# Placing a decoder trunk's buffers at multiples of 512 bytes, with raw pairs at a pitch of 272 columns

## The chip, the cores and the metric
The kernel runs on one core of a Trainium2 chip. A core has a matrix engine (PE, with its weight loads listed apart as PEld), a vector engine (DVE), a scalar engine (ACT), a general engine (POOL) and a queue engine (SP) that here issues every DMA. The metric is the device time of one launch in microseconds. Three runs of the kernel before took 624.08, 625.19 and 625.38 us, so the median is 625.19 us.

## The reference
A trunk of two layers over 256 positions of 1,024 features, in float32. Layer 0 mixes positions by causal attention with 8 heads of 128 (with 256 positions there is one block, so the block-sparse routing selects nothing beyond it), layer 1 by a gated causal convolution of width 3. After each mixer comes a SwiGLU with 2,816 hidden features. Each of the four sub-layers reads a normed and modulated residual and adds its result under a gate; shift, scale and gate come from the conditioning vector `c`.

```python
sc = silu(c)
for i in range(2):
    sh_m, sc_m, g_m, sh_f, sc_f, g_f = split(sc @ w_ada[i] + b_ada[i], 6)
    h = rms_norm(x, norm_mix[i]) * (1 + sc_m) + sh_m
    y = attention(h, w_qkv, w_o, q_gain, k_gain) if i == 0 else short_conv(h, w_in, conv_w, w_out)
    x = x + g_m * y
    h = rms_norm(x, norm_ffn[i]) * (1 + sc_f) + sh_f
    x = x + g_f * ((silu(h @ W_gate) * (h @ W_up)) @ w_down[i])
```

## The kernel before
The residual stands feature-major in `xT`: 8 tiles of 128 features by 256 positions. Every large product is made in three passes (`mm3`, lines 285 to 289): each float32 operand is split into a float32r part `h` and a remainder `l`, and PE computes h·h, h·l and l·h into the same accumulators. A pass is one matmul of a 128 by 128 block that PE loads and 256 columns that it streams; lines 287, 288 and 289 are the three passes of all large products.

The weights come in chunks of 1,024 rows by 256 columns (1 MB). SP loads a chunk into one of five buffers `wf`; ACT copies it into `wh` and DVE subtracts to get `wl` (lines 98 and 99), in two halves each, three buffers of both kinds. The list `chunks` sets their order; between them run the pieces of the modulation matrices (`wa`), which DVE multiplies and sums up (line 116). A scheduler places the instructions of the engines, except in the first stage, whose order is written by hand.

The stages in order of time: a first stage with the first modulation, queries and half of the keys (to some 57 us); keys, values and the attention's own steps; the output product `op_o`; the gate and up products of layer 0 (`pg`, `pu`, with the modulated pair `f0h`, `f0l`); the down products `op_d` (with the pair `a0h`, `a0l`, 22 rows); in layer 1 the convolution's products (`pc`, `pu`, `pb`, with `m1h`, `m1l`), `op_co`, and again gate, up and down (`f1`, `a1`).

The first products of three sub-layers don't wait for the norm. `Norm.take` writes a raw pair row by row as the residual's tiles come: 256 positions times scale, without the norm, and two more columns that hold the shift (lines 373 to 381). A row therefore has 258 columns, and the raw pair lies in the memory of `av` or of the wide pair: `raw_in` and `wide_pair` cut it out with rows of S + 2 columns. `raw_gemm` multiplies it, computes the norm's sum in between (lines 387 and 388) and applies it afterwards.

Tiles are placed in the order of their first use, one pool after the other, at multiples of 32 bytes in each partition. The constants before the weight pool end such that the first `wf` buffer starts at byte 20,448. Modulo 512, all `wf`, `wh` and `wl` buffers start at 480. The modulated pair (`m0`, `f0`, `m1`, `f1`: the same memory) starts at 32 in both halves, `a0h` and `a1h` at 96, `a0l` and `a1l` at 480, the wide pair (`ov`, `zv`) at 480 and 32, `xT` at 32. `ident_r`, with which `keep_warm` (line 566) keeps PE occupied early, starts at 256.

Of the kernel before, what the change touches and what calls it, by code (L numbers as in the profile page):

```python
# [8 lines left out]
F32 = mybir.dt.float32  # L9
# [6 lines left out]
P = 128  # L16
S = 256
D = 1024
KD = D // P
# [4 lines left out]
KF = D_FF // P  # L24
CW = 256
EPS = 1e-6
MASKED = -1e30
# [4 lines left out]
def trunk_kernel(ctx: ExitStack, tc: tile.TileContext, x, c, w_ada, b_ada, norm_mix, norm_ffn, w_qkv, w_o,  # L32
# [3 lines left out]
    const = ctx.enter_context(tc.tile_pool(name="const", bufs=1))  # L36
# [16 lines left out]

# [1 line left out]
    crow = const.tile([KD, P], F32, name="crow")  # L55
# [24 lines left out]

# [1 line left out]
    def load(src, nk, ncol, name):  # L82
# [17 lines left out]

# [1 line left out]
    mod = const.tile([P, DEPTH * 48], F32, name="mod")  # L102
    acc_of = {}
    late, gets = [], [0]

    def ada_piece(l, part, i):
        w = load(w_ada[l, i * 256:(i + 1) * 256, part * D:(part + 1) * D], 2, D, f"wa_{l}_{part}_{i}")
        if i == 0:
            acc_of[l, part] = tmp.tile([P, D], F32, tag="acc", name=f"acc_{l}_{part}", bufs=1)
        acc = acc_of[l, part]  # L110
        for kk in range(2):
            k = 2 * i + kk
            if k == 0:
                nc.vector.tensor_scalar(acc, w[:, kk], sc[:, k:k + 1], None, op0=ALU.mult)
            else:
                nc.vector.scalar_tensor_tensor(acc, w[:, kk], sc[:, k:k + 1], acc, op0=ALU.mult, op1=ALU.add)  # L116
        if i < 3:
            return
        if l == 0 and part != G_F:
            late.append((gets[0], lambda: ada_end(l, part, acc)))  # L120
            return
        # the sum over the partitions, of three bfloat16 parts that add up to the float32 values: less for PE
        parts = [tmp.tile([P, D], BF16, tag=f"part{n}", name=f"part{n}_{l}_{part}", bufs=1) for n in range(3)]
        for n, p in enumerate(parts):
            if n < 2:
                nc.scalar.activation(p, acc, AF.Copy)
                nc.vector.tensor_sub(acc if n == 0 else parts[2], acc, p)
        late.append((gets[0], lambda: ada_end_parts(l, part, parts)))

    def ada_end(l, part, acc):  # L130
        # the sum over the partitions, on four groups of 32 columns of the array at once: less for DVE and ScalarE
        ps = ps_misc(f"mod_ps_{l}_{part}")[:, :2 * P]
        for g in range(4):
            nc.tensor.matmul(ps[32 * g:32 * g + 32], one.to_broadcast([P, 32]), acc[:, g * 2 * P:(g + 1) * 2 * P],
                             start=True, stop=True, skip_group_check=True, tile_position=(0, 32 * g))
        y = tmp.tile([P, 2, P], F32, tag="t", name=f"mod_y_{l}_{part}", bufs=3)
        nc.scalar.activation(y, ps.rearrange("p (i c) -> p i c", c=P), AF.Copy)

        def end():
            ps = ps_misc(f"mod_c_{l}_{part}")  # L140
            for i in range(2):
                nc.tensor.transpose(ps[:, i * P:(i + 1) * P], y[:, i], ident)
            mod_from(ps[:, :2 * P].rearrange("p (i g r) -> p g i r", i=2, r=32)[:, :, :, 0], l, part)

        return end
# [43 lines left out]
    brow, vrow, grow = (rows[:n, i * P:(i + 1) * P] for i, n in enumerate((DEPTH * 48, 42, 16)))  # L189
    x_flat = act.tile([P, KD * (S + 2)], F32, tag="zh", name="x_tok")  # L190
    x_tok = x_flat[:, :2 * D].rearrange("p (t d) -> p t d", d=D)
# [16 lines left out]

# [1 line left out]
    chunks = []  # L210
# [72 lines left out]

# [1 line left out]
    def mm3(ps, lhs, rhs, first, last):  # L285
# [28 lines left out]

    # A raw pair holds x * (1 + scale) * gain, not yet over its norm, and the shift as one more token (twice, for an
    # even number of them). Products of it need no norm; rstd and the product of the shift come to them afterwards:
    # (x A rstd + sh) W = (x A) W rstd + sh W.
    RAW = KD * (S + 2)

    def wide_pair(name):  # L320
        flat = [act.tile([P, RAW], F32R, tag="z" + p, name=name + p) for p in "hl"]
        return (tuple(f[:, :KD * S].rearrange("p (k s) -> p k s", s=S) for f in flat),
                tuple(f.rearrange("p (k s) -> p k s", s=S + 2) for f in flat))

    def raw_in(pair):
        flat = [t.rearrange("p k s -> p (k s)") for t in pair]
        return tuple(f[:, KF * S - RAW:].rearrange("p (k s) -> p k s", s=S + 2) for f in flat)

# [1 line left out]
    xT = act.tile([P, KD, S], F32, name="xT")  # L330
# [20 lines left out]
    class Norm:  # L351
        """Sums of squares over the features, gathered as the residual's tiles come."""

# [83 lines left out]
    def raw_gemm(keys, norm, name):  # L437
        """Two chunks' products of the raw pair; returns (product * rstd, the shift's product) of each, and
        the modulated pair. The norm's own products come in between."""
        raw = norm.raw  # L440
        ada_ends()
        pss = [[psum.tile([P, S + 2], F32, tag=tag, name=f"raw_{name}_{i}{o}", bufs=n) for o in range(2)]
               for i, (tag, n) in enumerate((("gemm", 4), ("alt", 2)))]
        ws = [get(k) for k in keys]
        for k in range(KD):
            if k == 2:
                norm.rstd()
            if k == 4:
                rows = norm.rows()
                with tc.high_priority(400):  # L450
                    hs = modulated(norm.l, norm.sh, norm.scl, rows, name)
            for ps, (wh, wl) in zip(pss, ws):
                for o in range(2):
                    cs = slice(o * P, (o + 1) * P)
                    mm3(ps[o], (wh[:, k, cs], wl[:, k, cs]), (raw[0][:, k], raw[1][:, k]), k == 0, k == KD - 1)
        res = []
        for i, tag in enumerate("sa"):
            y = tmp.tile([P, 2, S], F32, tag=tag, name=f"rawy_{name}_{i}")
            b = tmp.tile([P, 2], F32, tag="rawb", name=f"rawb_{name}_{i}")
            for o in range(2):  # L460
                nc.vector.tensor_copy(b[:, o:o + 1], pss[i][o][:, S:S + 1])
                nc.vector.tensor_mul(y[:, o], pss[i][o][:, :S], rows)
            res.append((y, b))
        return res[0], res[1], hs
# [19 lines left out]

# [1 line left out]
    def mod_sums(w, name):  # L486
        # Four groups of 32 columns of the array hold four rows of c at once: partial sums in four groups of partitions.
        n = w.shape[1]
# [10 lines left out]
    def group_sums(ps, y, name):  # L499
        # the four groups' partial sums added up, as columns  # L500
        n = y.shape[1]
# [48 lines left out]
    def first_products(k, ops, js):  # L550
        wh, wl = ops
        for j in js:
            for t in range(2):
                ts = slice(t * P, (t + 1) * P)
                # q feature-major, k token-major
                if j < 4:
# [9 lines left out]
    def keep_warm(n):  # L566
        # The array's clock falls while it idles: products that nothing reads keep it up until the first operands are there.
        ps = ps_misc("warm")
# [4 lines left out]
    with tc.manual_schedule(engines={mybir.EngineType.PE, mybir.EngineType.DVE, mybir.EngineType.Activation}):  # L573
# [4 lines left out]
        nc.vector.tensor_copy(mask_r, causal)  # L578
        # brings the table of square roots in before the first one is needed
        std = const.tile([P, 2], F32, name="std0")  # L580
# [55 lines left out]

# [1 line left out]
    qT = act.tile([P, 2, H, S], F32, tag="ah", name="qkT")  # L638
# [25 lines left out]
    def q_sums(ps, a):  # L664
        # Four heads at once, on 32 columns of the array each: their sums end in four groups of partitions.
        for g in range(4):
# [73 lines left out]

    # The attention's own steps run between the products of the k and v chunks, each late enough to find its operands.
    ahead = get(("k", 2))
# [37 lines left out]

# [1 line left out]
    ups = [act.tile([P, 2, S + 2], F32, tag=f"up{i}", name=f"up{i}") for i in range(2)]  # L782
# [37 lines left out]

# [1 line left out]
    of = out[0].rearrange("(t p) d -> p t d", p=P)  # L822
# [43 lines left out]
```

## Time and profile before
| what | value |
|---|---|
| median of 3 runs | 625.19 us (624.08 to 625.38) |
| span of the profiled execution, from first to last instruction | 622.1 us |
| PE busy, share of the span | 609.7 us, 98% |
| DVE busy | 473.6 us, 76% |
| ACT busy | 323.1 us, 52% |
| DMA | 156.07 MB, mean 251 GB/s |

Busy time of PE is from the start of a matmul to its end, and matmuls overlap: one takes about 280 ns, but the next starts some 115 ns after it. What a stage costs is therefore read from the starts, or from how many matmuls lie in a window. The chain of waits names, from the end backwards, what each step waited for. The span leaves out what lies before the first and after the last instruction; the median of the runs is 3.1 us above it.

### The profile page before, as it was taken

The numbers are of one execution on the slowest core, as the hardware profiler recorded it, in microseconds if no ns is written. First come the engines' busy times: TensorE is split into PE (matmuls) and PEld (weight loads), VectorE is DVE, ScalarE is ACT, GpSimd is POOL, SyncE is SP. The second block draws the span as 40 slices with busy tenths as digits, with TensorE's granted clock in tenths as the row PEclk, the third lists the DMA queues.
The fourth block names the chain that finished last, engine by engine and source line by source line (L and its number), as shares of the span: only waits on it lengthen the run. The fifth ranks groups of instructions, "written<-read, shape, count | busy, mean of one in ns | idle before, by whom it ended". The sixth has DMA issues, their size and how long they took to land.

```text
span 622.1 us, 12512 instructions
## 1 busy us (share of the span) xinstructions
PE 609.7 (98%) x5291; PEld 595.8 (96%) x5291; DVE 473.6 (76%) x668; ACT 323.1 (52%) x518; POOL 19.2 (3%) x26
## 2 busy tenths in 40 slices
PE   7999999999999999999999999999999999999997
PEld 5789999999999999999999999998999999999997
DVE  5567999989989899979888989658976467644440
ACT  5335977466655455535355745545744435533330
POOL 0000000020000000000110000012000000000000
PEclk9999999999999999999999999999999999999999
DMA  9999999966699999798998497646388677655200
GB/s 271 329 331 354 385 370 335 303 219 223 210 323 322 347 333 335 257 318 303 319 302 278 133 304 241 210 138 205 108 299 271 201 225 235 204 188 178 94 18 17
DMA packets 127455, 156.07 MB, mean 251 GB/s; under 512 B 2822, under 2 KB 114856, under 8 KB 127400
## 3 DMA queue, kind: packets, MB, share of 16 engines
q1 hardware_dynamic: 127400, 155.28, 75.6%
q8 instruction: 41, 0.67, 0.5%
q14 instruction: 14, 0.11, 0.1%
HBM read 154.22 MB, written 1.05 MB: 250 GB/s over the span
## 4 chain that ended last, share of the span: by engine, by line
PE 88%; DMA 3%; DVE 3%; issue 3%; ACT 1%; SPq 0%; POOLq 0%; POOL 0%; ACTq 0%
PE pu L289 7%; PE pu L288 7%; PE op_d L287 7%; PE pu L287 7%; PE op_d L289 7%; PE op_d L288 7%; PE pg L289 6%; PE pg L288 6%; PE pg L287 6%; DMA wa<-in_w_ada_dram 2%; DMA wf_qk<-in_w_qkv_dram 1%; PE pv L287 1%; PE pb L288 1%; PE pv L289 1%; PE pb L287 1%
## 5 line engine op out<-in xcount | busy, mean ns | idle before, releaser
L116 DVE SCALAR_TENSOR_TENSOR acc<-wa,sc,acc 128x1024 f32<-128x1024 f32 x70 | 89.8, 1283 | 8.8 <-DMA wa<-in_w_ada_dram 7.5
L98 ACT ACTIVATE wh_d<-wf_d 128x1024 fp32r<-128x1024 f32 (+1 forms) x48 | 45.5, 981 | 69.7 <-issue 47.2
L99 DVE TENSOR_TENSOR wl_d<-wf_d,wh_d 128x1024 fp32r<-128x1024 f32 (+1 forms) x48 | 53.6, 1144 | 30.7 <-ACT wh_d L98 30.5
L98 ACT ACTIVATE wh_u<-wf_u 128x1024 fp32r<-128x1024 f32 x44 | 44.3, 1051 | 45.3 <-issue 34.5
L98 ACT ACTIVATE wh_g<-wf_g 128x1024 fp32r<-128x1024 f32 x44 | 45.5, 1050 | 40.7 <-issue 40.7
L99 DVE TENSOR_TENSOR wl_u<-wf_u,wh_u 128x1024 fp32r<-128x1024 f32 x44 | 52.7, 1233 | 14.0 <-ACT wh_u L98 14.0
L99 DVE TENSOR_TENSOR wl_g<-wf_g,wh_g 128x1024 fp32r<-128x1024 f32 x44 | 54.5, 1245 | 2.1 <-ACT wh_g L98 2.0
L287 PE MATMUL op_d<-a1h,wh_d 128*128 128x256 f32 x176 | 50.3, 286 | 0.0
L287 PE MATMUL op_d<-a0h,wh_d 128*128 128x256 f32 x176 | 50.2, 285 | 0.0
L289 PE MATMUL op_d<-a1h,wl_d 128*128 128x256 f32 x176 | 50.0, 284 | 0.0
L289 PE MATMUL op_d<-a0h,wl_d 128*128 128x256 f32 x176 | 50.0, 284 | 0.0
L288 PE MATMUL op_d<-a1l,wh_d 128*128 128x256 f32 x176 | 49.6, 282 | 0.0
L288 PE MATMUL op_d<-a0l,wh_d 128*128 128x256 f32 x176 | 49.5, 281 | 0.0
L289 PE MATMUL pg<-f1h,wl_g 128*128 128x256 f32 x160 | 44.8, 280 | 0.0
L289 PE MATMUL pu<-f1h,wl_u 128*128 128x256 f32 x160 | 44.8, 280 | 0.0
L287 PE MATMUL pg<-f1h,wh_g 128*128 128x256 f32 x160 | 44.6, 279 | 0.0
L288 PE MATMUL pg<-f1l,wh_g 128*128 128x256 f32 x160 | 44.6, 279 | 0.0
L287 PE MATMUL pu<-f1h,wh_u 128*128 128x256 f32 x160 | 44.6, 279 | 0.0
L288 PE MATMUL pu<-f1l,wh_u 128*128 128x256 f32 x160 | 44.6, 279 | 0.0
L287 PE MATMUL pg<-f0h,wh_g 128*128 128x256 f32 x160 | 44.5, 278 | 0.0
L289 PE MATMUL pg<-f0h,wl_g 128*128 128x256 f32 x160 | 44.4, 278 | 0.0
L289 PE MATMUL pu<-f0h,wl_u 128*128 128x256 f32 x160 | 44.4, 278 | 0.0
(315 smaller groups left out, 2103.6 us busy)
## 6 DMA issues: line engine op xcount, KB each, us to landing
wa<-in_w_ada_dram SPq DMA_DIRECT2D x40, 1024.0 KB, 6.1
wf_g<-in_w_gate_up_dram SPq DMA_DIRECT2D x22, 1024.0 KB, 6.6
wf_u<-in_w_gate_up_dram SPq DMA_DIRECT2D x22, 1024.0 KB, 7.5
wf_d<-in_w_down_dram SPq DMA_DIRECT2D x16, 1024.0 KB, 6.3
wa<-in_w_ada_dram SPq DMA_DIRECT2D x16, 512.0 KB, 7.1
wf_d<-in_w_down_dram SPq DMA_DIRECT2D x8, 768.0 KB, 5.7
wf_qk<-in_w_qkv_dram SPq DMA_DIRECT2D x8, 512.0 KB, 8.1
wf_v<-in_w_qkv_dram SPq DMA_DIRECT2D x4, 1024.0 KB, 7.5
```

The lines of the kernel that those rows point to most:

```text
L98: nc.scalar.activation(wh[:, a:b], wf[:, a:b], AF.Copy)
L99: nc.vector.tensor_sub(wl[:, a:b], wf[:, a:b], wh[:, a:b].bitcast(F32))
L116: nc.vector.scalar_tensor_tensor(acc, w[:, kk], sc[:, k:k + 1], acc, op0=ALU.mult, op1=ALU.add)
L287: nc.tensor.matmul(ps, ah, bh, start=first, stop=False, skip_group_check=True)
L288: nc.tensor.matmul(ps, ah, bl, start=False, stop=False, skip_group_check=True)
L289: nc.tensor.matmul(ps, al, bh, start=False, stop=last, skip_group_check=True)
```

## The change
A new constant tile of 32 bytes, which nothing writes or reads, pushes the weight pool to byte 20,480, a multiple of 512. The rows of the raw pairs get a pitch of SP = S + 16 = 272 columns (1,088 bytes) in place of 258 (1,032 bytes), of which the first 258 are used as before; by that the wide pair grows from 8,256 to 8,704 bytes a half, and everything behind it moves. Modulo 512, all of `wf`, `wh`, `wl`, the modulated pair, `a0`/`a1`, the wide pair and `xT` now start at 0, `ident_r` stays at 256, and the small tiles behind them start at multiples of 32 or 64. Comments are taken out too, so that lines of the changed kernel stand 3 lower down than those before (L381 becomes L384).

```diff
+SP = S + 16
...
     sc = const.tile([P, KD], F32, name="sc")
+    const.tile([P, 8], F32, name="pad")
...
-    x_flat = act.tile([P, KD * (S + 2)], F32, tag="zh", name="x_tok")
+    x_flat = act.tile([P, KD * SP], F32, tag="zh", name="x_tok")
...
-    RAW = KD * (S + 2)
+    RAW = KD * SP
     def wide_pair(name):
         flat = [act.tile([P, RAW], F32R, tag="z" + p, name=name + p) for p in "hl"]
         return (tuple(f[:, :KD * S].rearrange("p (k s) -> p k s", s=S) for f in flat),
-                tuple(f.rearrange("p (k s) -> p k s", s=S + 2) for f in flat))
+                tuple(f.rearrange("p (k s) -> p k s", s=SP)[:, :, :S + 2] for f in flat))
     def raw_in(pair):
         flat = [t.rearrange("p k s -> p (k s)") for t in pair]
-        return tuple(f[:, KF * S - RAW:].rearrange("p (k s) -> p k s", s=S + 2) for f in flat)
+        return tuple(f[:, KF * S - RAW:].rearrange("p (k s) -> p k s", s=SP)[:, :, :S + 2] for f in flat)
```

The order of instructions stays the same on PE, POOL and SP. On DVE and ACT the scheduler moves a few around the raw pairs of the two SwiGLU layers. The first place is DVE at the end of the attention's output product, before the change; `a0l<-mod` is the write of the shift columns, `xT<-op_o` a residual tile, `wl_u` half a weight split.

```order
199 L404 SCALAR_TENSOR_TENSOR xT<-op_o_2_1_1728,mod,xT 128x256
200 L99 TENSOR_TENSOR wl_u_0_1815<-wf_u_0_1812,wh_u_0_1814 128x1024
201 L374 SCALAR_TENSOR_TENSOR a0l<-xT,mod,a0h 128x256
202 L99 TENSOR_TENSOR wl_u_0_1815<-wf_u_0_1812,wh_u_0_1814 128x1024
203 L381 TENSOR_TENSOR a0l<-mod,a0h 128x8x2
204 L404 SCALAR_TENSOR_TENSOR xT<-op_o_3_0_1810,mod,xT 128x256
205 L374 SCALAR_TENSOR_TENSOR a0l<-xT,mod,a0h 128x256
206 L404 SCALAR_TENSOR_TENSOR xT<-op_o_3_1_1811,mod,xT 128x256
```

The same place on DVE after the change:

```order
199 L407 SCALAR_TENSOR_TENSOR xT<-op_o_2_1_1728,mod,xT 128x256
200 L102 TENSOR_TENSOR wl_u_0_1816<-wf_u_0_1813,wh_u_0_1815 128x1024
201 L377 SCALAR_TENSOR_TENSOR a0l<-xT,mod,a0h 128x256
202 L384 TENSOR_TENSOR a0l<-mod,a0h 128x8x2
203 L377 SCALAR_TENSOR_TENSOR a0l<-xT,mod,a0h 128x256
204 L102 TENSOR_TENSOR wl_u_0_1816<-wf_u_0_1813,wh_u_0_1815 128x1024
205 L407 SCALAR_TENSOR_TENSOR xT<-op_o_3_0_1811,mod,xT 128x256
206 L407 SCALAR_TENSOR_TENSOR xT<-op_o_3_1_1812,mod,xT 128x256
```

The shift columns and one row of the raw pair now stand ahead of the second half of the split, and the last two residual tiles behind it.

The second place is DVE at the end of the convolution's output product, before the change (`a1l<-mod` is the shift again):

```order
447 L404 SCALAR_TENSOR_TENSOR xT<-op_co_2_1_5196,mod,xT 128x256
448 L99 TENSOR_TENSOR wl_u_0_5272<-wf_u_0_5269,wh_u_0_5271 128x1024
449 L381 TENSOR_TENSOR a1l<-mod,a1h 128x8x2
450 L99 TENSOR_TENSOR wl_u_0_5272<-wf_u_0_5269,wh_u_0_5271 128x1024
451 L374 SCALAR_TENSOR_TENSOR a1l<-xT,mod,a1h 128x256
452 L404 SCALAR_TENSOR_TENSOR xT<-op_co_3_0_5267,mod,xT 128x256
453 L404 SCALAR_TENSOR_TENSOR xT<-op_co_3_1_5268,mod,xT 128x256
```

After the change, from the shift's new place on:

```order
440 L384 TENSOR_TENSOR a1l<-mod,a1h 128x8x2
441 L407 SCALAR_TENSOR_TENSOR xT<-op_co_0_0_5030,mod,xT 128x256
442 L407 SCALAR_TENSOR_TENSOR xT<-op_co_0_1_5031,mod,xT 128x256
443 L407 SCALAR_TENSOR_TENSOR xT<-op_co_1_0_5032,mod,xT 128x256
444 L102 TENSOR_TENSOR wl_co_5071<-wf_co_5068,wh_co_5070 128x1024 x2
445 L377 SCALAR_TENSOR_TENSOR a1l<-xT,mod,a1h 128x256 x3
446 L407 SCALAR_TENSOR_TENSOR xT<-op_co_1_1_5033,mod,xT 128x256
447 L407 SCALAR_TENSOR_TENSOR xT<-op_co_2_0_5196,mod,xT 128x256
448 L102 TENSOR_TENSOR wl_g_0_5201<-wf_g_0_5198,wh_g_0_5200 128x1024 x2
449 L377 SCALAR_TENSOR_TENSOR a1l<-xT,mod,a1h 128x256 x2
450 L407 SCALAR_TENSOR_TENSOR xT<-op_co_2_1_5197,mod,xT 128x256
451 L102 TENSOR_TENSOR wl_u_0_5273<-wf_u_0_5270,wh_u_0_5272 128x1024
```

The shift has left its place between the two halves of the split and stands ahead of the first residual tile.

## Rows read from the trace of the kernel before

**Rows 1.** Page, engines (busy, share, instructions) and the span in 40 slices.
```profile
PE 609.7 (98%) x5291; PEld 595.8 (96%) x5291; DVE 473.6 (76%) x668; ACT 323.1 (52%) x518; POOL 19.2 (3%) x26
...
PEclk9999999999999999999999999999999999999999
...
GB/s 271 329 331 354 385 370 335 303 219 223 210 323 322 347 333 335 257 318 303 319 302 278 133 304 241 210 138 205 108 299 271 201 225 235 204 188 178 94 18 17
```

**Rows 2.** Page, the chain that ended last, share of the span by engine.
```profile
PE 88%; DMA 3%; DVE 3%; issue 3%; ACT 1%; SPq 0%; POOLq 0%; POOL 0%; ACTq 0%
```

**Rows 3.** Windows: length, busy (instructions) of PE, PEld, DVE, ACT, POOL; clock, DMA, GB/s.
```profile
155.00:199.00 44.00, 44.00 (x375) 44.00 (x375) 40.93 (x48) 25.45 (x31) 0.00 (x0) 1.00 0.80 276
201.00:231.00 30.00, 30.00 (x268) 30.00 (x266) 27.45 (x27) 15.69 (x19) 0.00 (x0) 1.00 1.00 339
...
267.00:298.00 31.00, 31.00 (x261) 31.00 (x260) 28.00 (x31) 14.24 (x19) 0.89 (x1) 1.00 0.91 308
...
440.00:552.00 112.00, 112.00 (x954) 111.96 (x954) 75.69 (x81) 55.32 (x67) 0.00 (x0) 1.00 0.69 224
```

**Rows 4.** Timeline of PE: start, duration, line, operation, tiles, shapes, count.
```profile
199.36 0.75 PE L151 MATMUL mod_ps<-one_b,part 128*128 128x1 bf16 x24
...
200.17 0.28 PE L288 MATMUL pg<-f0l,wh_g 128*128 128x256 f32 x1
200.28 0.28 PE L289 MATMUL pg<-f0h,wl_g 128*128 128x256 f32 x1
```

**Rows 5.** Timeline of PE from 12.2 us, the warming products.
```profile
12.02 0.75 PE L570 MATMUL warm<-ident_r 128*128 128x256 f32 x5
```

**Rows 6.** Chain in order of time (start, duration), the queries' transposes.
```profile
66.31 0.44 PE q_cols L676 x4
```

**Rows 7.** Groups by form (busy, mean ns, idle before): ACT, raw rows and modulated rows.
```profile
L373 ACT ACTIVATE a0h<-xT,mod 128x256 fp32r<-128x256 f32 x8 | 3.9, 498 | 1.5 <-DVE a0l L381 1.5
...
L341 ACT ACTIVATE f0h<-t_f,mod 128x256 fp32r<-128x256 f32 x8 | 3.5, 498 | 1.6 <-DVE t_f L340 1.6
```

**Rows 8.** Timeline at the start of layer 0's raw products.
```profile
139.63 1.75 DVE L99 TENSOR_TENSOR wl_u<-wf_u,wh_u 128x1024 fp32r<-128x1024 f32 x1
139.74 0.22 ACT L380 ACTIVATE a0h<-mod 128x16 fp32r<-128x16 f32 x1 [1.30 <-DVE a0l L374]
...
141.30 0.17 DVE L381 TENSOR_TENSOR a0l<-mod,a0h 128x16 fp32r<-128x16 f32 x1
...
141.51 0.39 PE L288 MATMUL raw_f<-a0l,wh_g 128*128 128x258 f32 x1 [1.12 <-DVE a0l L381]
...
142.44 0.48 DVE L404 SCALAR_TENSOR_TENSOR xT<-op_o,mod,xT 128x256 f32<-128x256 f32 x1
...
143.62 0.40 ACT L359 ACTIVATE sq_n<-xT 128x256 f32<-128x256 f32 x1
...
144.37 0.28 PE L387 MATMUL ms_n<-inv_d,ss_n 128*128 128x1 f32 x2
```

**Rows 9.** Timeline at the start of layer 1's raw products.
```profile
424.20 0.70 DVE L381 TENSOR_TENSOR a1l<-mod,a1h 128x16 fp32r<-128x16 f32 x1
...
424.96 0.39 PE L288 MATMUL raw_f<-a1l,wh_g 128*128 128x258 f32 x1 [0.32 <-DVE a1l L381]
...
428.99 0.38 PE L387 MATMUL ms_n<-inv_d,ss_n 128*128 128x1 f32 x2 [1.04 <-POOL ss_n L367]
```

**Rows 10.** Chain in order of time, the loads of the start, first and last of three.
```profile
3.08 7.10 DMA wa<-in_w_ada_dram
...
14.71 9.28 DMA wf_qk<-in_w_qkv_dram
```

**Rows 11.** Chain, the first loop's modulation products, first and last of four.
```profile
33.92 1.07 PE mod_ps L493 x16
...
50.95 1.00 PE mod_ps L493 x16
```

**Rows 12.** Timeline, the first of these groups.
```profile
16.21 1.07 PE L493 MATMUL mod_ps<-wa,sc 128*32 128x256 f32 x16 [0.85 <-DMA wa<-in_w_ada_dram]
```

## The prediction
> **What bounds the kernel now.** I read the first parts of the page, then the chain, then stretches of single matmuls. PE is busy 98% of the 622.1 us span, with a granted clock of nine tenths or more in every slice [rows 1]. The chain that ended last is 88% PE, with 3% each of DMA, DVE and issue [rows 2]. So nearly everything hangs on one number, the step from the start of one matmul to the next, which I call the cadence. The durations that the groups print (about 280 ns) don't give it, since they overlap. Windows that lie inside one stage count the matmuls; length over count, with the two already under way at the window's start taken off, is the cadence [rows 3]:
> - gate and up products of layer 0, first part: 44.0 us / 373 = 118.0 ns; second part 30.0 / 266 = 112.8 ns;
> - down products of layer 0: 31.0 / 259 = 119.7 ns;
> - gate and up products of layer 1: 112.0 / 952 = 117.6 ns.
>
> [...] So there are three cadences, about 113, 118 and 120. The same products on the same buffers change from 118 to 113 within a stage: up to 199.36 us the step is 118 ns, then 24 small bfloat16 products interrupt the stream, and from 200.17 it is 0.11 us [rows 3, 4]. No address changed there, so at least that difference is the phase in which the stream was started.
>
> **The change, part by part.** Before, every large buffer starts at an odd multiple of 32 bytes: modulo 512 the weights at 480, the modulated pair at 32, the two halves of `av` at 96 and 480, those of the other wide pair at 480 and 32. After, all start at 0, and the rows of a raw pair step 1,088 bytes instead of 1,032. No arithmetic goes, and PE's order stays as it is. Time can move in four places.
>
> *PE's cadence.* The products of 256 or 258 float32r columns come from lines 287, 288 and 289; by the loops each issues 1,568, so 4,704 in all, and 1 ns of cadence is 4.7 us. What alignment does to one product is shown in one place: the warming products have `ident_r` (byte 256 modulo 512, before and after) on both sides, with 256 columns of the same type. The last five take 0.75 us [rows 5]; without the 0.28 of the last one four steps remain, 117.5 ns each. That is the cadence of the unaligned ones. On the other side stand transposes, whose loaded operand starts at an odd multiple of 32 and whose 128 float32 columns are aligned: four take 0.44 us, 110 ns each [rows 6]. I take 0 for the cadence, by the warming products, the one row with the right type and both operands aligned. For the ends I need a mean: with 576 products at 113, 1,056 down products at 119.7 and the other 3,072 at 118 it is 117.8. All at 113: 4,704 x 4.8 = -23 us. All at the transposes' 110: -37 us. All at 120: +10 us.
>
> *ACT and DVE.* The raw pair's rows started at every multiple of 8 bytes. ACT writes such a row (a0h) in 498 ns, and a row of an even pitch (f0h) in 498 ns too [rows 7]. Term: 0. If that were wrong, only the stages of the next part would see it, since PE waits for neither engine elsewhere.
>
> *Order.* The scheduler now puts the write of the shift columns (`a0l<-mod`, L381) ahead of half a weight split. At the end of the attention's output product PE waits 1.12 us for that write: DVE has the 1.75 us split from 139.63 in front of it, and it ends at 141.47 [rows 8]. In the new order it can start at 139.96, when ACT's part (139.74 + 0.22) is done. But then the split and the last two residual tiles stand behind it and behind the next `a0l` row, which itself needs a square (0.40) and a row (0.50) of ACT first, so that DVE gets to it at about 140.9. From there a row as long as a residual (0.48), the split (1.75 at most) and two residuals (0.48 each) end at 144.1 or a little sooner; before, the last one ended at 142.92. The norm's sum needs this tile and its square, 0.40 more, so it comes at about 144.5; before, PE reached it at 144.37 without a wait [rows 7, 8]. What is won ahead of the raw products is lost ahead of the norm: I take +0.1 us, with ends -1.1 (nothing late behind it) and +1.0 (a second step slowed). In layer 1 the shift leaves DVE's queue before the first residual: PE's wait of 0.32 us for it goes, and its 0.70 us no longer stands ahead of the last residuals, so that the norm's sum, for which PE waits 1.04 us, comes sooner [rows 9]. Term -0.4 us, ends -1.0 and 0.
>
> *DMA.* Every load lands at a new place. The chain runs through three DMA pieces from 3.08 us to 14.71 + 9.28 = 23.99 [rows 10]. Later PE sets the pace, 5.68 us for each step of the first loop (three from 33.92 to 50.95) [rows 11]. A faster load is therefore worth what lies before PE's own pace: up to 14.71, 11.6 us, and after that 33.92 - (16.21 + 3 x 5.68) = 0.7 us [rows 11, 12]. The first three slices moved 271, 329 and 331 GB/s, the best one 385 [rows 1]. At 385 instead of 331 the end is 11.6 x 0.14 + 0.7 = -2.3 us; loads 5% slower would be +0.6. I take 0: no row shows one kind of load at two places, and the nearest is the rate as it stands.
>
> The sum against the profiled execution: 622.1 + 0 + 0.1 - 0.4 + 0 = 621.8 us of span. The runs' median is 625.19, 3.1 above that span, and I let the 3.1 stand: 624.9 us.
>
> **Rivals.**
>
> *A. An odd start costs a fetch, and the cadence falls broadly.* [...] With 113 everywhere the time is 625 - 23 = 602, with 110 everywhere 588.
>
> [...]
>
> *B. The two reading streams collide.* PE reads the next weights while a product streams. Now weights and both moving halves have the same place modulo 512. Before, the modulated pair lay 64 bytes behind the weights in both halves, and its stages run at 113 or 118; the down products' halves lay 128 and 0 behind, and run at 120 [rows 3]. If 0 is the bad distance, all go to 120: +10 us, 635. It decides from the point where layer 0's second part loses its 113, which alone is 576 x 4.9 = +2.8 us, 627.7. Against it: the warming products have distance 0 and 117.5 ns [rows 5].
>
> *C. The phases fall anew.* No rule of place, but the stream starts otherwise after its interruptions. If the convolution's products (480) and the slow gate and up products (384 + 960) fall to 113, that is 1,824 x 4.9 = -8.9 us, 616; if the fast part is lost, 627.7. For it speaks the change of step at 200 us [rows 4].
>
> *D. Loads land faster*, and the start gains its 2.3 us: 622.6. The packed loop of the start is where it must show [rows 10 to 12].
>
> [...]
>
> **How the numbers follow.** A change under 0.2% (1.25 us) can't be told from none. Forecast, the cadences much as now with small changes of phase, 619 to 629: 0.42, of which 0.18 within 0.2%, 0.12 faster and 0.12 slower. A: 0.24, faster, 0.10 of it below 602. B: 0.13, slower, 0.04 of it above 632. C beyond the forecast's own range: 0.13, 0.07 faster and 0.06 slower. D: 0.08, 0.07 faster and 0.01 the same. Faster 0.50, same 0.19, slower 0.31. The range is 602 to 632: from A at 113 to B a little short of its end, with 0.14 left out.
>
> **What would show it.** In the new profile the same windows count the matmuls. By the forecast about 375 of them stand in the 44 us of layer 0's first part and 261 in the 31 us of down products. A shows as 276 or more in 31 us of down products. B shows as 261 or fewer in every 31 us of gate and up products. C shows as a step between 118 and 113 at an interruption, with the down products left at 120. D shows as the first loop's group at 16.21 us coming earlier. The order term is right if the wait for L381 is gone and one for the norm's sum of about its size stands some 3 us later. The prediction is wrong if the down products leave 120.

## The result, and the profile after

The changed kernel takes 631.27 us (median of 4 runs, 630.62 to 631.72); the kernel before took 624.63 on the same chip (4 runs, 623.91 to 625.38). The ratio is 1.0103, with a 95% interval of 1.0082 to 1.0125: slower by 1.0%. The profiled executions have spans of 629.5 and 622.1 us. All of the difference lies inside the span: every run's time is 1.8 us above its own span, before and after.

The first lines of the page of the changed kernel, against [rows 1] and [rows 2]: engines, the span in slices, the chain by engine.

```profile
PE 619.2 (98%) x5291; PEld 605.8 (96%) x5291; DVE 473.3 (75%) x668; ACT 321.2 (51%) x518; POOL 19.2 (3%) x26
...
PEclk9999999999999999999999999999999999999999
...
GB/s 287 352 345 375 358 331 310 327 197 201 226 316 325 347 314 314 259 288 295 320 297 286 127 304 253 184 133 195 146 293 268 192 220 236 207 184 170 101 18 17
...
PE 89%; issue 3%; DMA 3%; DVE 2%; ACT 1%; SPq 1%; POOL 0%; POOLq 0%; ACTq 0%
```

PE is busy as often as before, at a granted clock of nine tenths or more, with the same 5,291 matmuls, and yet for 9.5 us longer. So the matmuls come further apart. Counting them inside the stages shows by how much. Windows of the changed kernel, with the columns of [rows 3]: the two parts of layer 0's gate and up products, its down products, the gate and up products of layer 1.

```profile
156.00:200.00 44.00, 44.00 (x369) 44.00 (x369) 39.71 (x47) 24.60 (x30) 0.00 (x0) 1.00 0.80 272
203.00:233.00 30.00, 30.00 (x253) 30.00 (x252) 26.63 (x27) 14.91 (x18) 0.00 (x0) 1.00 0.98 332
...
275.00:293.00 18.00, 18.00 (x152) 18.00 (x151) 15.96 (x17) 8.93 (x12) 0.91 (x1) 1.00 0.86 282
...
446.00:558.00 112.00, 112.00 (x936) 112.00 (x935) 74.88 (x81) 54.44 (x66) 0.00 (x0) 1.00 0.67 221
```

With two taken off each count, the steps are 119.9, 119.5, 120.0 and 119.9 ns; before they were 118.0, 112.8, 119.7 and 117.6 [rows 3]. By the single starts in the trace it is 120.0 ns in all four, at the granted clock of 1.00 that the windows show; the down products before were at 120.0 by their starts too. No stage of the changed kernel has a stream at 118 or 113 ns any more.

From the starts of the first product of each stage, in the two traces (us):

| stage | before | after | difference |
|---|---|---|---|
| start to the first product of `k_2` | 61.6 | 60.7 | -0.9 |
| keys and values | 50.8 | 51.7 | +0.9 |
| `op_o` | 27.6 | 27.5 | -0.1 |
| raw products of layer 0 | 14.1 | 14.5 | +0.4 |
| gate and up, layer 0, to the interruption | 45.8 | 46.7 | +0.9 |
| gate and up, layer 0, from there | 66.7 | 70.5 | +3.8 |
| down products, layer 0 | 64.7 | 64.7 | 0.0 |
| convolution, raw and other products | 69.9 | 71.0 | +1.1 |
| `op_co` | 23.1 | 23.1 | 0.0 |
| raw products of layer 1 | 14.5 | 13.7 | -0.8 |
| gate and up, layer 1 | 113.7 | 115.8 | +2.1 |
| down products of layer 1 and the end | 69.5 | 69.6 | +0.1 |

The sum is +7.4, all of what the spans differ by. The loss sits in the stages that ran below 120 ns; the down products and `op_co`, at 120 already, lost nothing.

Waits of PE at the raw products, and what DVE does ahead of them (timeline of the changed kernel, against [rows 8]; the last line answers to [rows 9]):

```profile
139.70 0.70 DVE L384 TENSOR_TENSOR a0l<-mod,a0h 128x16 fp32r<-128x16 f32 x1
...
140.46 0.39 PE L291 MATMUL raw_f<-a0l,wh_g 128*128 128x258 f32 x1 [0.26 <-DVE a0l L384]
...
141.86 0.86 DVE L407 SCALAR_TENSOR_TENSOR xT<-op_o,mod,xT 128x256 f32<-128x256 f32 x2
...
144.49 0.38 PE L390 MATMUL ms_n<-inv_d,ss_n 128*128 128x1 f32 x2 [1.02 <-POOL ss_n L370]
...
434.18 0.38 PE L390 MATMUL ms_n<-inv_d,ss_n 128*128 128x1 f32 x2 [0.70 <-POOL ss_n L370]
```

The wait for the shift fell from 1.12 to 0.26 us, and four us later stands a wait of 1.02 for the norm's sum that wasn't there. In layer 1 the wait for the shift is gone and that for the sum fell from 1.04 to 0.70.

The rest that the prediction rested on: the chain's loads of the start, its modulation products and the queries' transposes (against [rows 10], [rows 11], [rows 6]), the first loop's group in the timeline (against [rows 12]), and two groups by form (against [rows 7]).

```profile
3.71 8.02 DMA wf_qk<-in_w_qkv_dram
...
13.46 8.28 DMA wa<-in_w_ada_dram
...
32.83 1.00 PE mod_ps L496 x16
...
49.98 1.00 PE mod_ps L496 x16
...
65.47 0.44 PE q_cols L679 x4
```

```profile
15.59 1.07 PE L496 MATMUL mod_ps<-wa,sc 128*32 128x256 f32 x16 [0.18 <-DMA wa<-in_w_ada_dram]
```

```profile
L376 ACT ACTIVATE a0h<-xT,mod 128x256 fp32r<-128x256 f32 x8 | 3.9, 495 | 0.0
...
L344 ACT ACTIVATE f0h<-t_f,mod 128x256 fp32r<-128x256 f32 x8 | 3.5, 498 | 1.6 <-DVE t_f L343 1.6
```

The chain's last load ends at 21.74 instead of 23.99 us, and the last modulation product of the loop stands at 49.98 instead of 50.95. ACT's rows and the transposes are as they were.

### The profile page after: what moved, and what is told of

Read it like the earlier page. It is cut to its first block, busy times and chain, and to the rows that moved or that the text cites. A ratio compares the mean times of both kernels' runs of the same rounds, so it can differ in the third digit from the quotient of the medians.

```text
span 629.5 us, 12518 instructions
## 1 busy us (share of the span) xinstructions
PE 619.2 (98%) x5291; PEld 605.8 (96%) x5291; DVE 473.3 (75%) x668; ACT 321.2 (51%) x518; POOL 19.2 (3%) x26
## 4 chain that ended last, share of the span: by engine, by line
PE 89%; issue 3%; DMA 3%; DVE 2%; ACT 1%; SPq 1%; POOL 0%; POOLq 0%; ACTq 0%
PE pu L291 7%; PE pu L290 7%; PE pu L292 7%; PE op_d L290 7%; PE op_d L292 7%; PE op_d L291 7%; PE pg L290 6%; PE pg L291 6%; PE pg L292 6%; PE pv L290 1%; DMA wa<-in_w_ada_dram 1%; DMA wf_qk<-in_w_qkv_dram 1%; PE pv L292 1%; PE pb L291 1%; PE pb L290 1%
## 5 line engine op out<-in xcount | busy, mean ns | idle before, releaser
L290 PE MATMUL pu<-f0h,wh_u 128*128 128x256 f32 x160 | 45.3, 283 | 0.0
L291 PE MATMUL pu<-f0l,wh_u 128*128 128x256 f32 x160 | 45.3, 283 | 0.0
L291 PE MATMUL pg<-f0l,wh_g 128*128 128x256 f32 x160 | 45.3, 283 | 0.0
```

What stands on the lines that cost most here:

```text
L290: nc.tensor.matmul(ps, ah, bh, start=first, stop=False, skip_group_check=True)
L291: nc.tensor.matmul(ps, ah, bl, start=False, stop=False, skip_group_check=True)
```

## The experiments

Theory 1, which rival B named: the place of the moving operand relative to the weights in the memory decides the cadence. Against it theory 2 (the absolute start decides), theory 3 (phases fall anew with any change) and the pitch or the order of DVE's work as the cause. Cadences are written as the step from start to start.

**Only the pad, only the pitch.**

```diff
 e1: before, and
+    const.tile([P, 8], F32, name="pad")
 e2: after, and
-    const.tile([P, 8], F32, name="pad")
```

> The kernel before with the 32-byte pad alone; the raw rows keep their pitch of 258 columns. All buffers from the weight pool on move by 32 bytes together: weights at 0 modulo 512, modulated pair at 64, a0h at 128, a0l at 0, wide pair at 0 and 64. The places of the two streams relative to each other are those of before. Theory 1 (the distance between the weights and the moving operand decides the cadence, and 0 is the bad one): the cadences of before return, 113 and 118 ns in the gate and up stages, 120 in the down products, and the time is that of before, 624.6 us, or up to 1.2 us less if the start's loads gain from the aligned landing place: 623.4 to 625. Theory 2 (a start at a multiple of 64 bytes is the bad one, an odd multiple of 32 the good one): every stream at 120 ns, 631. Theory 3 (the phases fall anew with any change): steps between 113 and 120 at other places than before, 618 to 631.

> The changed kernel without the pad: the pitch of 272 columns stays, and everything from the weight pool on lies 32 bytes lower, all of it at 480 modulo 512. The distance between weights and moving operand is 0 in every stage, as in the changed kernel, but every start is an odd multiple of 32. Theory 1 (distance 0 is bad): every stream at 120.0 ns, 631 us, or 632.5 if the start loses what the aligned loads gave. Theory 2 (odd multiples of 32 are good): 113 to 118 ns in the gate and up stages, 624 to 625. Theory 3 (phases fall anew): steps between 113 and 120 at other places, 618 to 631. If the pitch or the order of DVE's shift write were the cause, this kernel would be slow at unchanged cadences, with the time in waits at the raw products.

Measured: e1 624.12 us, ratio to before 0.9996 (0.9982 to 1.001). e2 634.02 us, ratio 1.0147 (1.0128 to 1.0165). Windows of e1, then of e2, in stretches that lie inside the same four stages in both:

```profile
156.00:196.00 40.00, 40.00 (x342) 40.00 (x341) 37.09 (x42) 22.26 (x28) 0.00 (x0) 1.00 0.85 295
205.00:229.00 24.00, 24.00 (x206) 24.00 (x205) 22.65 (x23) 13.17 (x16) 0.00 (x0) 1.00 0.97 329
275.00:293.00 18.00, 18.00 (x152) 18.00 (x151) 17.01 (x19) 9.03 (x13) 0.90 (x1) 1.00 0.84 282
448.00:538.00 90.00, 90.00 (x767) 90.00 (x766) 61.12 (x60) 42.60 (x51) 0.00 (x0) 1.00 0.72 239
```

```profile
156.00:196.00 40.00, 40.00 (x336) 40.00 (x335) 36.11 (x48) 24.76 (x31) 0.00 (x0) 1.00 0.77 256
205.00:229.00 24.00, 24.00 (x203) 24.00 (x202) 20.84 (x21) 12.25 (x15) 0.00 (x0) 1.00 0.98 340
...
448.00:538.00 90.00, 90.00 (x752) 90.00 (x751) 62.52 (x68) 44.17 (x54) 0.00 (x0) 1.00 0.72 230
```

e1: 117.6, 117.6, 120.0, 117.6 ns. e2: 119.8, 119.4 and 120.0. With every start at an even multiple of 32 but the old distances, e1 is not slow; with every start at an odd multiple and distance 0, e2 is. Theory 2 falls, and the pad alone, with the pitch and order of before, costs nothing. One thing theory 1 alone didn't say: in e1 the second part of layer 0 runs at 117.6, not at the 113 of before. The distance allows a fast step; whether it comes depends on more. So e1's time is that of before as a balance: its second part costs 2.5 us more, and its start takes 1.9 us less. e2's span is 2.8 us longer than that of the changed kernel: 1.4 of it lies before `k_2`, where the loads decide, and 1.5 in the raw products of layer 0. There the granted clock falls. Windows of these products, e2 and then the changed kernel:

```profile
148.15:151.10 2.95, 2.95 (x16) 2.95 (x15) 2.07 (x3) 0.00 (x0) 0.00 (x0) 0.51 0.70 231
```

```profile
144.50:149.00 4.50, 4.50 (x38) 4.50 (x39) 3.65 (x6) 2.13 (x4) 0.00 (x0) 1.00 0.76 276
```

In e2 the products between 148.15 and 151.10 us step 0.21 us at a granted clock of 0.51, some 2 us after PE had waited 1.03 us for the norm's sum. The changed kernel waits 1.02 us at the same place, and its clock stays at 1.00; why it falls in one and not in the other is not shown. This loss is not one of places, and it is why e2 lies above its 632.5.

**The cadence by itself.** Two scans with nothing but products, so that no other engine and no load takes part. Offsets are written as (weights h, weights l, moving h, moving l), where "weights" is the operand that PE loads. The loops, shortened:

```diff
+    for wh, wl, xh, xl in offsets:            # slices of four regions
+        for breaks in (24, 8, 1, 3):          # e3: 8, 24, 1
+            ...                               # small bfloat16 products
+            ...                               # 12 (e3: 16) times the passes wh.xh, wh.xl, wl.xh
```

> Leaves out the whole computation of the reference and measures the cadence by itself: streams of 48 float32r products in the kernel's three passes (h.h, h.l, l.h; 128 by 128 weights, 256 columns), in regions that start at multiples of 4096 bytes, with nothing else running. 32 sets of offsets of the four operands, each in three streams that begin after 8, 24 and 1 small bfloat16 products. Theory 1: 120 ns at distance 0 (also 512 and 1024, and at any common offset such as 480 or 32), 113 to 118 at 64; the sets with one half at 0 and the other at 64 or 128 lie between. Theory 2: 120 at all even multiples of 32, 113 to 118 at the odd ones whatever the distance. Theory 3: the three streams of one set differ among themselves as much as the sets do. Total some 32 x 3 x 48 products x 0.113 to 0.120 us = 520 to 555 us plus some 30 us for filling the regions.

> Leaves out the computation of the reference, as the scan before it. Streams of 36 float32r products in the three passes, with the weights' h half at 0 modulo 256 and the weights' l half and both moving halves at each of 0, 64, 128 and 192: 64 sets, each begun after 24, 8, 1 and 3 small bfloat16 products. Theory 1 in the sharper form that the first scan gives (120.0 ns at any distance that is a multiple of 256, 117.8 or 113.3 at 64, 192, 320 and 448 by the phase of the start, and 113.3 in two of three starts where the l half of the weights lies 128 behind the h half): 120.0 at (0, 0, 0, 0) in all four starts; other sets between 113 and 120, some with two steps by the start; if one set gives 113.3 in all four starts, it is the place to choose. A theory by which only the mean distance counts would give the sets with the same sum the same step.

Single matmuls, from the sixth to the last of a stream each: e3 with (0, 0, 0, 0) and then (0, 0, 64, 64), both after 1 small product.

```profile
586.11 0.28 PE L109 MATMUL c31s<-regions 128*128 128x256 f32 x1
...
591.15 0.28 PE L109 MATMUL c31s<-regions 128*128 128x256 f32 x1
...
78.03 0.28 PE L109 MATMUL c3s<-regions 128*128 128x256 f32 x1
...
82.98 0.28 PE L109 MATMUL c3s<-regions 128*128 128x256 f32 x1
```

Over 42 steps that is 120.0 and 117.9 ns (117.8 by the starts in ns). e4, where 30 steps lie between the rows: (0, 0, 192, 192) after 24 and after 3 small products, then (0, 128, 192, 192) after 24.

```profile
286.26 0.28 PE L141 MATMUL c15s<-regions 128*128 128x256 f32 x1
...
289.80 0.28 PE L141 MATMUL c15s<-regions 128*128 128x256 f32 x1
...
299.41 0.28 PE L141 MATMUL c15s<-regions 128*128 128x256 f32 x1
...
302.81 0.28 PE L141 MATMUL c15s<-regions 128*128 128x256 f32 x1
...
871.50 0.28 PE L141 MATMUL c47s<-regions 128*128 128x256 f32 x1
...
874.90 0.28 PE L141 MATMUL c47s<-regions 128*128 128x256 f32 x1
```

118.0 (117.8 in ns), 113.3 and 113.3. The steps of the sets that matter, by the starts in ns, one number for each start of a stream (the very first stream of a scan is left out):

| offsets | steps, ns |
|---|---|
| both moving halves 0, 256, 512, 1024 behind weights at 0; also all at 32, all at 480; also (0, 0, 96, 96) | 120.0 in every start |
| (0, 0, 64, 64), and the same at 480 and 32 | 117.8 in every start |
| (0, 0, 320, 320) | 117.8, 117.8, 113.3 |
| (0, 0, 192, 192) | 117.8, 117.8, 113.3, 113.3 |
| (0, 0, 128, 0), the set of the old down products | 118.9 to 119.6 (120.0 in the kernel) |
| (0, 128, 64, 64) | 113.3, 118.9, 113.3, 113.3 |
| (0, 128, 192, 192) | 113.3 in all four |
| (0, 128, 192, 128), (0, 192, 0, 192) | 120.0 in all four |
| (0, 128, 192, 64) | 120.9, 120.8, 120.9, 120.9 |

Theory 1 holds, sharpened in three ways. The distance counts modulo 256, not 512. The place of the l half counts too, so equal places are one bad set, neither the only one nor the worst. And one set can have two steps that hold once they have begun: the phase of theory 3 is real, inside the bounds that the places set. In the kernels distance 64 has both steps as well, 117.8 and 113.3 in before. A mean distance does not decide: (0, 0, 0, 128), (0, 0, 64, 64) and (0, 0, 128, 0) have one sum and steps of 116.7, 117.8 and about 119. What is not shown is what inside the memory or PE collides.

**Whole kernels by the scan.**

```diff
 e6: after, and
+    act.tile([P, 16], F32, name="pad_act")     # ahead of all of act: every moving pair at 64
 e8: after with SP = S + 8, and
+    act.tile([P, 48], F32, name="pad_act")     # every moving pair at 192
 e5: after with SP = S + 8, and
+    act.tile([P, 16], F32, name="pad_act")     # with the next line, moving pairs at 192
+    wpool.tile([P, 32], F32, name="pad_wl")    # between wh and wl: wl at 128
```

> The changed kernel with the one set of places that took 113.3 ns in all four starts of the second scan: modulo 256 the weights' h half at 0, their l half at 128 (a 128-byte pad between the two), both halves of every moving pair at 192 (a 64-byte pad before them); the pitch is 264 instead of 272 columns, since the room is needed. Theory 1 (the relative places decide): all 3,840 products of 256 columns with the weights loaded from wh and wl outside the start go from 120.0 to 113.3 ns, that is -25.6 us against the changed kernel, 605.7, and up to 1.5 us more from keys, values and the start: 604 to 606. Theory 3 (phases fall anew, no rule of place): somewhere between 113 and 120 at random, 612 to 631. A rival by which another engine or the loads take over once PE is faster: the cadence inside the streams is 113.3, but gaps grow and the time stops short of 606, at 608 to 615.

> The changed kernel with one pad of 64 bytes ahead of all activation buffers: the weights stay at 0 modulo 512, every moving pair goes from 0 to 64. Pitch and order stay those of the changed kernel. Theory 1: no stream stays at 120 but the raw products; 117.8 ns by seven of seven starts in the scans, so 3,840 x 2.2 = -8.6 us against the changed kernel: 622.7; where a start falls into 113.3, less. Theory 2 (a start at an even multiple of 32 is bad): 120 everywhere, 631. If the pitch or the changed order had cost the 6.6 us: 631.

> As the kernel with the best set of places, but the weights' l half back at 0 modulo 256: weights 0 and 0, moving pairs 192. In the scans this set took 113.3 ns after 1 and 3 small products and 117.8 after 8 and 24, so here the phase of each start should decide. Theory 1 with phases: each uninterrupted stretch at either 113.3 or 117.8 ns, none at 120 but the raw products; all at 117.8 would be 607.65 + 3,840 x 4.45 ns = 624.7 (less where stretches fall into 113.3), all at 113.3 would be 607.65. If the l half's place had nothing to do with the gain of the best set: 607 to 609 with 113.3 everywhere.

Measured: e6 622.74 us, ratio 0.9975 (0.9962 to 0.9988); e8 614.74, ratio 0.9848 (0.9816 to 0.9881); e5 607.65, ratio 0.9736 (0.9714 to 0.9758). Windows of e6, two of the four stages:

```profile
156.00:196.00 40.00, 40.00 (x342) 40.00 (x342) 36.26 (x43) 22.62 (x28) 0.00 (x0) 1.00 0.83 285
...
275.00:293.00 18.00, 18.00 (x155) 18.00 (x154) 17.12 (x19) 9.39 (x13) 0.90 (x1) 1.00 0.88 293
```

117.6 ns each, now in the down products as well. 64 bytes ahead of the activations, with pitch and order untouched, turn the changed kernel's loss into a small gain; that settles that neither pitch nor order had cost it. That e6 meets its 622.7 is in part luck: in its trace the products win 9.7 us and the start 0.9, and the raw products lose 1.9, most of it in layer 1, where the granted clock is 0.50 from 429.2 to 432.3 us. Windows of e8 on both sides of an interruption in layer 0's gate and up products, and the interruption:

```profile
205.00:229.00 24.00, 24.00 (x206) 24.00 (x205) 22.16 (x22) 13.55 (x16) 0.00 (x0) 1.00 0.98 334
...
233.25 0.75 PE L154 MATMUL mod_ps<-one_b,part 128*128 128x1 bf16 x24
...
235.00:261.00 26.00, 26.00 (x232) 26.00 (x231) 22.64 (x24) 13.19 (x16) 0.00 (x0) 1.00 0.83 273
```

117.6 ns before it and 113.0 behind it, on the same buffers: this is the picture of [rows 3, 4] again. The interruption at 198.63 us had left e8 at 117.8. Its six runs range from 612.79 to 619.88 us, wider than those of any other kernel here; that phases fall otherwise from run to run would fit, but only one of them has a trace. Windows of e5, the four stages:

```profile
154.00:195.00 41.00, 41.00 (x364) 41.00 (x363) 37.44 (x45) 24.67 (x30) 0.00 (x0) 1.00 0.80 273
199.00:229.00 30.00, 30.00 (x267) 30.00 (x267) 26.64 (x26) 16.31 (x19) 0.00 (x0) 1.00 0.97 330
275.00:293.00 18.00, 18.00 (x161) 18.00 (x161) 17.86 (x20) 10.43 (x14) 0.90 (x1) 1.00 0.98 334
448.00:538.00 90.00, 90.00 (x797) 90.00 (x796) 59.64 (x58) 43.38 (x52) 0.00 (x0) 1.00 0.72 236
```

113.3, 113.2, 113.2, 113.2 ns. The l half's place takes the luck out of these stages: between e8 and e5 only it changed. The keys' and values' products stay at 117.8 ns; in them PE loads the activations and streams the weights, so their set is another one. e5 beats the kernel before by 2.6%, and it missed its expectation of 604 to 606 by 1.7 us. A new wait, 1.44 us for a value that DVE makes behind a piece whose load is late, shows where (timeline of e5, raw products of the convolution):

```profile
331.30 1.28 DVE L119 SCALAR_TENSOR_TENSOR acc<-wa,sc,acc 128x1024 f32<-128x1024 f32 x1 [2.40 <-DMA wa<-in_w_ada_dram]
332.50 0.16 DVE L397 RECIPROCAL rs_n<-sd_n 128x2 f32<-128x2 f32 x1
...
332.81 0.40 PE L339 MATMUL rr_n<-ident,rs_n 128*128 128x128 f32 x2 [1.44 <-DVE rs_n L397]
```

So the rival that the loads take over once PE is faster is true here, at one place.

**Where the loads land.**

```diff
 e7: before, with wf alone moved from 480 to 0
+    const.tile([P, 8], F32, name="pad")
+    wpool.tile([P, 120], F32, name="pad_wh")   # between wf and wh
 e9: after, with wf alone moved from 0 to 480
-    const.tile([P, 8], F32, name="pad")
+    wpool.tile([P, 8], F32, name="pad_wh")
```

> The kernel before with the landing buffers wf alone moved, from 480 to 0 modulo 512 (pads of 32 bytes ahead of them and of 480 behind them); all that PE reads keeps its place modulo 512, and the pitch stays 258. By the landing theory (rival D of the prediction: loads into aligned buffers are faster) the first four slices of the page show some 290 350 350 380 GB/s instead of 271 329 331 354, and the product loop of the start comes 1.5 to 2 us earlier: 622.5 to 623, or about 625 if the second part of layer 0's gate and up products loses its 113 ns by a change of phase (2.6 us). If the landing place doesn't matter: 624.6, slices as before.

> The changed kernel with the landing buffers wf alone put back to 480 modulo 512; all that PE reads stays at 0, the pitch stays 272. By the landing theory the first four slices return to some 272 330 330 357 GB/s and the product loop of the start comes 1 to 1.5 us later: 632.3 to 634.0, every stream at 120.0 ns. If the start's gain in the changed kernel came from anything but the landing place: 631.3 and slices of 287 352 345 375.

Measured: e7 622.56 us, ratio 0.9966 (0.9953 to 0.9978); e9 633.67, ratio 1.0147 (1.0122 to 1.0172). The slices of the page, e7 and then e9:

```profile
GB/s 301 357 356 358 339 369 305 316 217 206 228 338 306 348 336 331 256 320 305 313 300 276 137 305 244 202 137 204 116 294 269 203 229 239 195 188 177 95 18 17
```

```profile
GB/s 277 327 330 361 385 358 309 309 220 203 211 314 321 351 326 304 260 292 288 328 291 283 130 312 243 187 134 196 146 299 267 188 220 232 214 182 174 98 18 17
```

The first three slices move 301, 357, 356 GB/s into buffers at 0 (e7) where before moved 271, 329, 331 into buffers at 480 [rows 1]; put back to 480 (e9) they move 277, 327, 330 where the changed kernel moved 287, 352, 345. That is 4 to 11%. The product stage of `k_2` starts 1.0 us earlier in e7 than in before, and 1.0 us later in e9 than in the changed kernel; every later stage has the same length within 0.05 us in both pairs, and the spans of the profiled executions differ by 1.0 us both times. The ratios give more, 0.3 and 0.4% (2.1 and 2.7 us), but they go with the mean granted clock of the runs: beside e9, before takes 623.7 to 624.1 us at 0.998 or more, 625.1 to 625.5 at 0.996 or 0.997, and 626.7 at 0.993 or 0.994. At 0.998 or more, the medians of e7 and of before beside it are 622.5 and 623.8 us, those of e9 and of the changed kernel 632.3 and 631.3: differences of 1.3 and 1.0. I take 1 us. e1, with `wf` at 0 as well, gains 1.9 us in its start; its other 0.9 us are not explained.

**Is there a faster set?**

> Leaves out the computation of the reference. The 448 sets of places left in a grid of 32 bytes (weights' h half at 0, their l half and both moving halves at 0 to 224 modulo 256, at least one of them an odd multiple of 32), in streams of 24 products after 8 small ones. Asks whether any set lies below 113.3 ns. [...]

As e4, with 24 products for each set. The first set's stream, the first of the launch, is left out. None of the other 447 lies below 113.3 ns; the lowest step is 115.3, and some 410 lie between 116.5 and 119.5. Three sets lie above 120.5, up to 122.2, and 30 within half a ns of 120. The sets were started once each, so one that has a faster phase may have been missed. The floor seen is 113.3: no stream of 256 float32r columns in e3, e4 or e10 stepped faster.

## Why the prediction was wrong

*The failed step* is "I take 0 for the cadence, by the warming products". The cadence went to 120 ns in every stage. From the table above, the stages that had been faster pay 0.9 + 0.9 + 3.8 + 1.1 + 2.1 = 8.8 us, and the loop of the start pays some more inside its own gain. The prediction's end for that, "All at 120: +10 us", was right in size, a little high because its mean took 118 ns for the 288 raw products and the 192 of `op_co`, which ran at about 120 before; the forecast put the likeliest value at the other row.

Why that row misled: its few steps are still 117 to 119 ns in the changed kernel, where every long stream is at 120.0, so it was never a measure of them. It reads the same 128 columns twice from the place of its own weights, and four steps of it, read with the rounding of the page, don't tell 118 from 120. And the first steps of a stream can differ from its later ones: behind the interruption at 200.47 us the changed kernel's starts, from 201.09 us on, are 202, 121, 117 and 117 ns apart, and 120 from there. Which of these made the difference is not shown. A row with the right type and alignment, but not the loop's access pattern, was given more weight than four stages with thousands of products.

*Rival B came true*, with its fit: the stages at distance 64 lost, and the down products had nothing to lose. So the sign by which the prediction called itself wrong, the down products leaving 120, did not come, and the forecast failed all the same. Its deciding point, the second part of layer 0, was priced at +2.8 us by a fall to 118; it fell to 120 and cost 3.8. Its distance was taken modulo 512 and is modulo 256. Its picture of one bad distance was too simple, by the sets of e4. Its objection, the warming products at distance 0, was the same misread row.

*Rival A fell.* An odd start costs nothing by itself: e2 (all odd) and after (all even) have the same cadence, 119.4 to 120.0 ns by their windows. What decides between 113.3, 117.8 and 120.0 ns is the places together, not one start.

*Rival C* is half of the truth: phases exist (e8), but after a move to distance 0 there is only one, 120.0.

*Rival D came true in its mechanism*: landing at 0 instead of 480 modulo 512 makes the start's loads faster, e7 and e9 by 4 to 11% in the slices. Its end was -2.3 us; the profiled executions of e7 and e9 show 1.0. The sign that it named does not tell: the first loop's group comes at 15.59 us instead of 16.21 in the changed kernel, but at 17.09 in e7, which is ahead only from the third group on. Why a landing at 0 is faster is not shown. Taking 0 for this term was off by that 1 us, to the good side.

*The order terms* were right in kind. In layer 0 the waits are 0.26 + 1.02 = 1.28 us where one of 1.12 stood: +0.16, forecast +0.1. In layer 1 the two waits of 0.32 and 1.04 became one of 0.70: -0.66, forecast -0.4. ACT and DVE at 0 was right (495 and 498 ns).

*The time around the span.* The 3.1 us that the prediction let stand were two things: 1.8 us outside the span, in every run, and 1.3 us by which the profiled execution was faster than the median.

## What to carry to other kernels

A stream of matmuls that is bound by PE has a cadence worth measuring from starts, stage by stage; several values for one shape (113, 118 and 120 ns before) mean that something besides the shape sets it. Here it is the place of the moving operand and of both weight halves relative to each other, modulo 256 bytes: equal places are a bad choice (120.0 ns; the best set took 113.3), and a few pads of 32 to 128 bytes, found by two scans, gave 17.6 us of 625, about 1 of them by the landing. Aligning the landing buffers of loads is a separate gain (1.0 us of span in e7 and in e9), so place what DMA writes and what PE reads each by what its own runs show.

## What the runs showed of the hardware

- Streams of 256 float32r columns ran at 113.3 to 122.2 ns (e3, e4, e10, mean granted clock 0.997 to 1.0), by the places of four operands modulo 256 bytes, most of them near 118, and the sets with all four at one place (0, 32, 480) at 120.0 in every start.
- Sets such as (0, 0, 192, 192) have two stable steps, 117.8 and 113.3; 24 bfloat16 products between can switch one into the other (e8, and before at 200 us).
- No set of the scans ran below 113.3 ns, and only (0, 128, 192, 192) of the 64 at multiples of 64 bytes ran so in all four starts.
- Loads into buffers at 0 modulo 512 moved 301, 357, 356 GB/s at the start (e7), into buffers at 480 271, 329, 331 (before).
- A stretch of 2.95 us at a granted clock of 0.51 cost e2 some 1.5 us; runs of before fall into groups about 1.4 us apart by their mean granted clock.
